# The second head's scores from tokens that are not normed, and block-wise transposes, in a two-block model's expert layer

## The chip, the cores and the metric

The kernel runs on one core of a Trainium2 chip as one launch. The metric is the device time of the run in microseconds (us), the median of several runs. TensorE multiplies matrices and transposes, VectorE (DVE in the profile) and ScalarE (ACT) work on vectors, GpSimd (POOL) issues the gathers of expert rows, and SyncE (SP) issues the loads of weights. All of them run at once and wait for one another through semaphores.

## What is computed

256 tokens of 1024 values pass through two blocks. Both blocks mix the tokens; the second ends with a layer of retrieved experts, and the change touches its beginning. In the reference, cut to what matters:

```
x  = x + gt1 * (concat(mla, mlstm) @ w_out)
h2 = rmsnorm(x, g_norm2) * (1 + sc2) + sh2
x  = x + gt2 * peer(h2, ...)

def peer(h, w_pq, sub_keys, expert_u, expert_v):        # per token
    q = (h @ w_pq).reshape(heads=8, 2, 128)
    s = einsum(q, sub_keys)                              # 2 x 128 scores per head
    sv, si = top_k(s, 16)                                # per half
    best, pos = top_k(sv[0] + sv[1], 16)                 # of 16 x 16 sums
    eidx = (si[0] * 128 + si[1])[pos]                    # 16 experts per head
    g = softmax(best)
    act = gelu(einsum(expert_u[eidx], h))
    return einsum(g * act, expert_v[eidx])
```

So each token has 8 heads with 16 experts each. An expert's row of u and its row of v, 1024 values each, lie side by side in memory.

## The kernel before

**Layout.** `XT` holds the tokens transposed: 8 tiles `k` of 128 features by 256 tokens. For the dot products with gathered rows, tokens must lie on partitions; the kernel calls that form `hn[b]`, one tile of 128 x 1024 for each of the two blocks `b` of 128 tokens. Matrix products at full precision are split in two parts: a weight `w` becomes `wh` (copied by ScalarE, L323) and `wl` (the rest, by VectorE, L268), the tokens become `hh` and `hl`, and `mm3` issues three matmuls for one product. A projection for one head has 2 halves x 8 tiles x 3 = 48 matmuls of 128x256, and its sub-scores are 4 more of 128x128 against the sub-keys (`sk0`, `sk`).

**The first head's way round the norm.** `second` (L1460 to L1516) ends the second block's mixing with `project(1)`, which finishes `XT` two tiles at a time. Behind each it splits these tiles, scaled by the gain only, into `xh` and `xl`. The first head's projection `ua` uses those, so it need not wait for the norm: the scores are linear, so the norm factor `y` of each token is multiplied in afterwards and what the shift adds is computed apart, as a bias. The bias is 16 matmuls of the weights against the shift column (`bp`, fp32) and 2 matmuls against sub-keys (`kp`), before `project(1)` ends. The result goes into a dead part of the constant tile `cst` (`sca0`) by two multiply-adds, which the trace shows as `cst<-s,ny,pc` (L262).

**The expert stage.** `peer` (L1518 to L1790) first finds 8 experts of head 0 in block 0 (`fast`, up to `found`; indices in `eix`), and the gathers begin. Then `normed` writes the normed tokens into a tile `t` that takes one of the 9 buffers `G`, and makes `hh` and `hl` from it; `natural` turns both blocks into `hn` with 32 matmuls against the identity; `scores(1)` follows; `residual` transposes `XT` in 16 transposes into `xn` for the end. `experts` runs 16 rounds (`r`), 16 experts each: round `r` handles head `r % 8` of block `r // 8`. One expert is one indirect DMA of 128 rows of 8 KB (L1685, buffer `G`), a dot product on VectorE (L1689), gelu on ScalarE for four at a time, and, in pieces of 128x512, 2 products of `dg` and `G` on TensorE that accumulate in PSUM. A gather can start when a buffer `G` is free, that is when the products of the expert nine before it are done. `scores(r + 2)` for the next heads is issued in round `r`, the routing of later rounds is handed out between dots (`side`).

**What sets the order.** `at(us)` gives a step a planned time, and a list scheduler orders each engine's instructions by these times and by its own model of when inputs are ready. Weight loads are asked for some time ahead (`wload`, 5 buffers `w`, 3 buffers each for `wh` and `wl`). `tc.issue_after` keeps a step behind another in the order. Each engine and each DMA queue then runs its list strictly in that order.

## Time and profile before

| | |
|---|---|
| median of 3 runs | 1378.23 us (1377.91 to 1381.11) |
| the profiled execution | 1375.42 us |
| its span in the trace | 1373.6 us |
| TensorE busy | 1197.5 us, 87% |
| VectorE busy | 994.4 us, 72% |
| ScalarE busy | 533.6 us, 39% |
| GpSimd busy | 292.5 us, 21% |

The profiled execution is 1.8 us longer than its span and 2.8 us shorter than the median. The shares of busy time are means over stages: in the span's first half TensorE and VectorE alternate, in its second half the DMA engines move the expert rows. The rows below are to be read stage by stage.

### The profile page before, as it was taken

To read this page: it belongs to the slowest core of one execution; us is meant where nothing else is said; L and a number is where in the kernel's file an instruction comes from. 1 tells how busy PE (TensorE), PEld (TensorE's weight loads), DVE (VectorE), ACT (ScalarE), POOL (GpSimd) and SP (SyncE) were. 2 spreads that over 40 slices of the span, in tenths; PEclk is the share of its full clock that TensorE was granted. 3 is DMA by queue.
4 is the path that set the end of the run, shared out by engine and by line. 5 is a ranking of instruction groups with operands and counts; after the bars stand their busy time and mean duration, and the time that the engine had idled before them with its cause. 6 is when DMAs were issued, how large, how long until landed. Compare 5 with 4: busy or idle time off the path is not lost.

```text
span 1373.6 us, 17829 instructions
## 1 busy us (share of the span) xinstructions
PE 1197.5 (87%) x6008; PEld 781.7 (57%) x6008; DVE 994.4 (72%) x2464; ACT 533.6 (39%) x1147; POOL 292.5 (21%) x279
## 2 busy tenths in 40 slices
...
GB/s 333 196 284 270 157 183 173 196 163 260 139 41 100 154 131 77 153 16 36 108 382 381 376 426 428 425 426 361 427 412 426 427 426 418 423 426 404 421 427 275
DMA packets 71483, 387.64 MB, mean 282 GB/s; under 512 B 8417, under 2 KB 9569, under 8 KB 38370
## 3 DMA queue, kind: packets, MB, share of 16 engines
q0 software_dynamic: 36864, 268.45, 46.9%
...
q8 instruction: 48, 0.79, 0.2%
...
HBM read 385.43 MB, written 1.05 MB: 281 GB/s over the span
## 4 chain that ended last, share of the span: by engine, by line
PE 49%; DMA 28%; issue 9%; DVE 8%; POOL 5%; ACT 2%; POOLq 0%; DVEq 0%; SPq 0%; ACTq 0%
DMA G<-uv,eix 23%; PE acc L256 22%; PE acx L256 10%; PE s L256 5%; POOL G L1685 5%; DVE G L1689 3%; PE o L256 2%; DMA wm<-wada 2%; PE c L256 2%; PE c L966 2%; PE t L256 1%; DMA w<-wpq 1%; PE t L259 1%; PE s L412 1%; PE o L645 1%
## 5 line engine op out<-in xcount | busy, mean ns | idle before, releaser
L1689 DVE SCALAR_TENSOR_TENSOR G<-G,hn 128x1024 f32<-128x1024 f32 x256 | 313.4, 1225 | 162.3 <-DMA G<-uv,eix 158.8
L1685 POOL DMA_INDIRECT G<-uv,eix x256 | 284.9, 1113 | 415.6 <-PE o L256 129.5
L323 ACT ACTIVATE wh<-w 128x1024 fp32r<-128x1024 f32 (+2 forms) x140 | 146.4, 1048 | 180.6 <-PE acc L256 111.0
L268 DVE TENSOR_TENSOR wl<-w,wh 128x1024 fp32r<-128x1024 f32 (+2 forms) x140 | 168.8, 1209 | 65.4 <-ACT wh L323 63.8
L256 PE MATMUL t<-G,dg 128*128 128x512 f32 x256 | 149.3, 668 | 62.9 <-ACT dg L1702 62.9
L256 PE MATMUL c<-G,dg 128*128 128x512 f32 x256 | 145.9, 654 | 49.2 <-ACT dg L1702 49.2
L256 PE MATMUL acc<-hh,wh 128*128 128x256 f32 x592 | 173.5, 297 | 6.0 <-ACT hh L468 2.5
L256 PE MATMUL acc<-hh,wl 128*128 128x256 f32 x592 | 173.0, 295 | 2.0 <-DVE wl L268 2.0
L256 PE MATMUL acc<-hl,wh 128*128 128x256 f32 x592 | 164.3, 288 | 1.1 <-DVE hl L268 1.1
L1702 ACT ACTIVATE dg<-cst,w 128x128 f32<-128x128 f32 x256 | 90.1, 395 | 141.7 <-PE acx L256 61.4
L256 PE MATMUL acx<-G,dg 128*128 128x512 f32 x256 | 143.3, 644 | 0.0
L256 PE MATMUL o<-G,dg 128*128 128x512 f32 x256 | 141.1, 635 | 0.0
L1693 ACT ACTIVATE s<-s 128x4 f32<-128x4 f32 (+1 forms) x66 | 13.5, 205 | 306.7 <-DVE G L1689 306.7
L256 PEld LDWEIGHTS t<-G,dg 128*128 128x128 f32 x256 | 50.9, 209 | 142.3 <-ACT dg L1702 87.6
L256 PEld LDWEIGHTS acc<-hh,wh 128*128 128x128 f32 x592 | 115.7, 196 | 14.8 <-issue 4.6
L256 PEld LDWEIGHTS acc<-hh,wl 128*128 128x128 f32 x592 | 115.9, 196 | 8.6 <-issue 4.3
L256 PEld LDWEIGHTS c<-G,dg 128*128 128x128 f32 x256 | 49.5, 206 | 117.0 <-ACT dg L1702 68.5
L262 DVE SCALAR_TENSOR_TENSOR g<-lu,pb,g 128x256 f32<-128x256 f32 x264 | 115.1, 478 | 0.2
L256 PEld LDWEIGHTS acc<-hl,wh 128*128 128x128 f32 x592 | 111.3, 192 | 5.3 <-issue 3.4
L256 PEld LDWEIGHTS acx<-G,dg 128*128 128x128 f32 x256 | 53.5, 209 | 70.7 <-issue 70.7
L256 PEld LDWEIGHTS o<-G,dg 128*128 128x128 f32 x256 | 52.7, 206 | 69.0 <-issue 68.8
L1057 POOL MEMSET lu<- 128x16 f32 x1 | 0.4, 441 | 399.3 <-DVE g L262 399.3
...
## 6 DMA issues: line engine op xcount, KB each, us to landing
w<-w SPq DMA_DIRECT2D x64, 512.0 KB, 4.4
wm<-wada SPq DMA_DIRECT2D x40, 512.0 KB, 4.3
wa<-cw SPq DMA_DIRECT2D x16, 512.0 KB, 5.0
w<-woa SPq DMA_DIRECT2D x16, 512.0 KB, 3.5
w<-wpq SPq DMA_DIRECT2D x14, 512.0 KB, 4.5
w<-w2t SPq DMA_DIRECT2D x12, 512.0 KB, 3.5
w<-wob SPq DMA_DIRECT2D x8, 512.0 KB, 3.5
w<-w2v SPq DMA_DIRECT2D x8, 512.0 KB, 3.8
```

The source lines that it names most:

```text
L256: return pe.matmul(out, lhsT, rhs, start=start, stop=stop)
L259: pe.transpose(out, in_, ident)
L262: return (e or dve).scalar_tensor_tensor(out, a, s, b, op0=op0, op1=op1)
L268: return (e or dve).tensor_tensor(out, a, b, op=op)
L323: act.activation(hi, w, AF.Copy)
L412: pe.matmul(acc[j:j + 32], ones[:, 0:32], sq[:, q] if square else srcs[i + q], start=i + q < 4, stop=i + q >= n - 4, tile_position=(0, j))
L645: pe.matmul(hps[32 * j:32 * j + 32], blk[:, q4 * 4 + j], w[:, j], start=q4 == 0, stop=q4 == 3, tile_position=(0, 32 * j))
L966: pe.matmul(acc[32 * j:32 * j + 32], sc[:, k], w[:, j], start=k == 0, stop=k == 7, tile_position=(0, 32 * j))
L1685: pool.indirect_dma_start(out=G, out_offset=None, in_=A["uv"], in_offset=bass.IndirectOffsetOnAxis(ap=eix[b][:, h, k:k + 1], axis=0))
L1689: dot = dve.scalar_tensor_tensor(G[:, 0:D], G[:, 0:D], 1.0, hn[b], op0=mul, op1=mul, accum_out=s[:, j:j + 1])
L1693: act.activation(s[:, 0:n], s[:, 0:n], AF.Gelu)
L1702: act.activation(dg, ident, AF.Copy, scale=w[:, j:j + 1])
```

## The change

The second head's scores are now computed as the first head's: a bias (16 matmuls against the shift column, 2 against sub-keys; `bias(1, ...)`, with its own load of the two weights, which are loaded once more for the split), a projection of `xh` and `xl` that is placed behind the first head's scores, and two multiply-adds with the norm factor (`rs2`), whose result overwrites the mask part of `cst`. `sk0` holds 4 rows of sub-keys instead of 2. `scores(1)` is gone from `peer`, and `sca` has room for 6 heads.

The first head's two multiply-adds come after all its four sub-score matmuls. The first two splits of the second head's weights stand behind the last split of `XT`.

`normed` returns the normed tokens `t`, with the shift added in place; `halves` makes `hh` and `hl` from them two tiles at a time, behind all of `fast`. `natural(0, tokens)` transposes block 0's tokens directly (8 transposes instead of 16 matmuls), and block 1 is turned by `natural(1)` at round 3 with 16 matmuls. `residual` runs for block 0 at round 2 and for block 1 at round 4, back into the cells of `XT` that it read; `finish` reads them there.

```
@@ -944,3 +944,4 @@
 
-    sca0 = cst[:, CN["cos2"][0]:CN["sin2"][1]].rearrange("p (b q n) -> p b q n", b=2, q=2)
+    sca0 = [cst[:, CN[n][0]:CN[n][0] + 512].rearrange("p (b q n) -> p b q n", b=2, q=2) for n in ("cos2", "cmask")]
+    kb = [None, cst[:, CN["ltri"][0]:CN["utri"][1]].rearrange("p (q n) -> p q n", q=2)]
 
@@ -1460,4 +1461,4 @@
         at(X + 93)
-        sk0 = slot("cw2", 256).rearrange("p (q n) -> p q n", q=2)
-        nc.sync.dma_start(sk0, A["subk"][:, 0:2])
+        sk0 = slot("cw2", 512).rearrange("p (q n) -> p q n", q=4)
+        nc.sync.dma_start(sk0, A["subk"][:, 0:4])
         w0 = [wload(A["wpq"][q], [128, 8, 128], "wm", NWM, b1) for q in range(2)]
@@ -1465,13 +1466,19 @@
         w0l = slot("lu", 2048, F32R).rearrange("p (q k n) -> p q k n", q=2, k=8)
-        bp = psum("s", [128, 2])
-        for q in range(2):
-            for k in range(8):
-                mm(bp[:, q:q + 1], w0[q][:, k], modt[:, 24 + k, 0:1], k == 0, k == 7)
-        b0 = mk(b1, [128, 2], tag="nv4")
-        act.activation(b0, bp, AF.Copy)
-        kp = psum("s", [128, 2, 128])
-        for q in range(2):
-            mm(kp[:, q], b0[:, q:q + 1].broadcast_to([128, 128]), sk0[:, q], True, True)
-        kb = slot("pc", 256).rearrange("p (q n) -> p q n", q=2)
-        act.activation(kb, kp, AF.Copy)
+        kb[0] = slot("pc", 256).rearrange("p (q n) -> p q n", q=2)
+        b0 = mk(b1, [128, 4], tag="nv4")
+
+        def bias(h, w):
+            bp = psum("s", [128, 2])
+            for q in range(2):
+                for k in range(8):
+                    mm(bp[:, q:q + 1], w[q][:, k], modt[:, 24 + k, 0:1], k == 0, k == 7)
+            act.activation(b0[:, 2 * h:2 * h + 2], bp, AF.Copy)
+            kp = psum("s", [128, 2, 128])
+            for q in range(2):
+                i = 2 * h + q
+                mm(kp[:, q], b0[:, i:i + 1].broadcast_to([128, 128]), sk0[:, i], True, True)
+            act.activation(kb[h], kp, AF.Copy)
+
+        bias(0, w0)
+        bias(1, [wload(A["wpq"][2 + q], [128, 8, 128]) for q in range(2)])
         for q in range(2):
@@ -1488,3 +1495,3 @@
                 act.activation(xh[:, k], XT[:, k], AF.Copy, scale=gk)
-                stt(xl[:, k], XT[:, k], gk, xh[:, k].bitcast(F32), mul, sub)
+                last = stt(xl[:, k], XT[:, k], gk, xh[:, k].bitcast(F32), mul, sub)
             at(X + 100 + 2.6 * (n + 1))
@@ -1504,10 +1511,25 @@
                     mm(ua[q], w0h[:, q, k], xl[:, k], False, k == 7)
-        qs = slot("ow", 512).rearrange("p (q t) -> p q t", q=2)
-        for q in range(2):
-            act.activation(qs[:, q], ua[q], AF.Copy)
-        sp = psum("s", [128, 2, 2, 128])
-        for b in range(2):
+
+        def head(h, qs, acc):
+            qs = slot(qs, 512).rearrange("p (q t) -> p q t", q=2)
             for q in range(2):
-                mm(sp[:, b, q], qs[:, q, b * 128:b * 128 + 128], sk0[:, q], True, True)
-            stt(sca0[:, b], sp[:, b], y[:, b:b + 1], kb, mul, add)
+                act.activation(qs[:, q], acc[q], AF.Copy)
+            sp = psum("s", [128, 2, 2, 128])
+            for b in range(2):
+                for q in range(2):
+                    held = mm(sp[:, b, q], qs[:, q, b * 128:b * 128 + 128], sk0[:, 2 * h + q], True, True)
+            return sp, held
+
+        sp, held = head(0, "ow", ua)
+        stt(sca0[0][:, 0], sp[:, 0], y[:, 0:1], kb[0], mul, add)
+        at(X + 116)
+        first_splits.extend([last.ins] * 2)
+        acc = psum("acc", [128, 2, T])
+        for q in range(2):
+            wh, wl = wsplit(A["wpq"][2 + q], [128, 8, 128])
+            with tc.issue_after(held.ins):
+                mm3(acc[:, q], [(wh[:, k], wl[:, k], xh[:, k], xl[:, k]) for k in range(8)])
+        mg["sp"] = head(1, "kv", [acc[:, q] for q in range(2)])[0]
+        at(X + 135)
+        stt(sca0[0][:, 1], sp[:, 1], y[:, 1:2], kb[0], mul, add)
         hh = mk(cp, [128, 8, T], F32R, tag="hh")
@@ -1536,3 +1558,3 @@
         gat = [mk(pp, [128, 8, 16], tag=f"gat{b}") for b in range(2)]
-        sca = mk(pp, [128, 7, 2, 2, 128], tag="sca")
+        sca = mk(pp, [128, 6, 2, 2, 128], tag="sca")
 
@@ -1552,3 +1574,3 @@
                     mm(sp[:, b, q], qs[:, q, b * 128:b * 128 + 128], sk[:, 2 * h + q], True, True)
-            act.activation(sca[:, h - 1], sp, AF.Copy)
+            act.activation(sca[:, h - 2], sp, AF.Copy)
 
@@ -1564,20 +1586,25 @@
                 stt(t[:, k], XT[:, k], mg["pr"][:, k:k + 1], bc, mul, mul)
-                sh = modt[:, 24 + k, 0:1]
-                act.activation(hh[:, k], t[:, k], AF.Identity, bias=sh)
-            for k in range(8):
-                stt(hl[:, k], t[:, k], modt[:, 24 + k, 0:1], hh[:, k].bitcast(F32), add, sub)
+                act.activation(t[:, k], t[:, k], AF.Identity, bias=modt[:, 24 + k, 0:1])
+            return t
 
-        def natural():
+        def halves(t):
+            for k in range(0, 8, 2):
+                act.activation(hh[:, k:k + 2], t[:, k:k + 2], AF.Copy)
+                tt(hl[:, k:k + 2], t[:, k:k + 2], hh[:, k:k + 2].bitcast(F32), sub)
 
-            for b in range(2):
-                for d in range(2):
-                    acc = pst("u", [128, 4, 128])
-                    for k in range(4):
+        def natural(b, t=None):
+
+            bs = slice(b * 128, b * 128 + 128)
+            for d in range(2):
+                acc = pst("u", [128, 4, 128])
+                for k in range(4):
+                    if t is None:
                         for i, x in enumerate((hh, hl)):
-                            last = mm(acc[:, k], x[:, d * 4 + k, b * 128:b * 128 + 128], identr, i == 0, i == 1)
-                    act.activation(hn[b][:, d * 512:d * 512 + 512], acc.rearrange("p a b -> p (a b)"), AF.Copy)
-            return last
+                            mm(acc[:, k], x[:, d * 4 + k, bs], identr, i == 0, i == 1)
+                    else:
+                        tr(acc[:, k], t[:, d * 4 + k, bs], ident)
+                act.activation(hn[b][:, d * 512:d * 512 + 512], acc.rearrange("p a b -> p (a b)"), AF.Copy)
 
         def subscores(h, b, p):
-            return sca0[:, b, p] if h == 0 else sca[:, h - 1, b, p]
+            return sca0[h][:, b, p] if h < 2 else sca[:, h - 2, b, p]
 
@@ -1657,13 +1684,11 @@
 
-        xn = XT.rearrange("p k t -> p (k t)").rearrange("p (b d) -> p b d", b=2)
 
-        def residual(held):
-            xp = [pst("v", [128, 4, 128]) for _ in range(4)]
-            for b in range(2):
-                for k in range(8):
-                    with tc.issue_after(held.ins):
-                        tr(xp[b * 2 + k // 4][:, k % 4], XT[:, k, b * 128:b * 128 + 128], ident)
-            for i in range(4):
-                act.activation(xn[:, i // 2, (i % 2) * 512:(i % 2) * 512 + 512],
-                               xp[i].rearrange("p a b -> p (a b)"), AF.Copy)
+        def residual(b):
+
+            for d in range(2):
+                xp = pst("u", [128, 4, 128])
+                cells = XT[:, 4 * d:4 * d + 4, b * 128:b * 128 + 128]
+                for k in range(4):
+                    tr(xp[:, k], cells[:, k], ident)
+                act.activation(cells, xp, AF.Copy)
 
@@ -1718,4 +1743,6 @@
         with tc.issue_after(found.ins):
-            normed()
-        at(B + 7)
+            tokens = normed()
+            for b in range(2):
+                stt(sca0[1][:, b], mg["sp"][:, b], rs2[:, b:b + 1], kb[1], mul, add)
+        at(B + 3)
         with tc.issue_after(found.ins):
@@ -1723,8 +1750,8 @@
                 placed = ins
-        at(B + 8)
-        held = natural()
-        first_splits.extend([found.ins] * 2)
-        scores(1, B + 9)
-        at(B + 16)
-        residual(held)
+        at(B + 4)
+        natural(0, tokens)
+        at(B + 6)
+        with tc.issue_after(placed.ins):
+            halves(tokens)
+        first_splits.extend([placed.ins] * 2)
 
@@ -1751,3 +1778,4 @@
                 yield 1
-                tt(o, o, xn[:, b, d * 512:d * 512 + 512], add)
+                o4 = o.rearrange("p (k n) -> p k n", k=4)
+                tt(o4, o4, XT[:, 4 * d:4 * d + 4, b * 128:b * 128 + 128], add)
                 nc.sync.dma_start(A["out"][b * 128:b * 128 + 128, d * 512:d * 512 + 512], o)
@@ -1760,2 +1788,8 @@
                 side.append(gate_sums())
+            if r in (2, 4):
+                at(U0 + 16 * PICK * r)
+                residual(r // 2 - 1)
+            if r == 3:
+                at(U0 + 16 * PICK * r)
+                natural(1)
             if r == 10:
@@ -1763,3 +1797,3 @@
             if r < 6:
-                scores(r + 2, U0 + 16 * PICK * r - 12)
+                scores(r + 2, U0 + 16 * PICK * r - (12 if r else -2))
             experts(r % 8, r // 8, U0 + 16 * PICK * r, 4 if r == 0 else 2, (4, 4, 4, 4) if r < 15 else (4, 4, 4, 2, 1, 1))
```

**TensorE, from the end of the mixing to the tokens, before.** `s_7125` are the token sums of the norm, `s_7197` the first head's sub-scores, `t_7250` the spread of the norm factor, and `acc_7317` and `acc_7327` the first of `natural`'s matmuls.

```order
L256 MATMUL s_7125<-cst_62,tmp_7123 128x1 x2
L256 MATMUL s_7197<-cw_1188_6916,ow_7194 128x128 x4
L256 MATMUL t_7250<-dg_7251,cst_62 128x128
L256 MATMUL t_7250<-dg_7254,cst_62 128x128
L256 MATMUL acc_7317<-identr_7213,hh_7204 128x128
L256 MATMUL acc_7327<-identr_7213,hh_7204 128x128
```

**The same place after, its first part.** `s_7151` are the token sums and `s_7223` the first head's sub-scores.

```order
L256 MATMUL o_7171<-g_1202_6979,g_1191_6922 128x256
L256 MATMUL s_7151<-cst_62,tmp_7149 128x1 x2
L256 MATMUL s_7223<-cw_1188_6916,ow_7220 128x128 x4
L256 MATMUL acc_7229<-g_1201_6978,wh_7232 128x256
L256 MATMUL acc_7229<-g_1202_6979,wh_7232 128x256
L256 MATMUL acc_7229<-g_1201_6978,wl_7234 128x256
```

The rows `acc_7229` go on for 48 matmuls, the second head's projection. This is the end of it, and what follows:

```order
L256 MATMUL acc_7229<-g_1202_6979,wh_7262 128x256
L256 MATMUL acc_7229<-g_1201_6978,wl_7264 128x256
L256 MATMUL s_7293<-cw_1188_6916,kv_7290 128x128 x4
L256 MATMUL t_7345<-dg_7346,cst_62 128x128
L256 MATMUL t_7345<-dg_7349,cst_62 128x128
L259 MATMUL acc_7406<-cst_62,G_7352 128x128 x4
L259 MATMUL acc_7412<-cst_62,G_7352 128x128 x3
L256 MATMUL acc_7430<-hh_7299,wh_7433 128x256
```

The spread of the norm factor, `t_7345`, now stands behind 48 matmuls and the second head's sub-scores `s_7293`; `natural`'s matmuls have become 8 transposes, and `acc_7430`, the projection of the third head, follows them.

**TensorE up to the first expert, before.** `acc_7454` is the third head's projection, `acx_7429` are the last of `residual`'s transposes, and `c_7523` is the first expert's first product.

```order
L256 MATMUL acc_7454<-hh_7204,wh_7487 128x256
L256 MATMUL acc_7454<-hl_7205,wh_7487 128x256
L256 MATMUL acc_7454<-hh_7204,wl_7489 128x256
L259 MATMUL acx_7429<-cst_62,XT_61 128x128 x3
L256 MATMUL c_7523<-G_7528,dg_7567 128x512
L256 MATMUL o_7524<-G_7528,dg_7567 128x512
```

**The same place after.** `acc_7717` is the fourth head's projection, `acc_7963` transposes of `residual(0)`, `s_7780` the fourth head's sub-scores, `acc_7969` the fifth head's projection.

```order
L256 MATMUL acc_7717<-hl_7300,wh_7750 128x256
L256 MATMUL acc_7717<-hh_7299,wl_7752 128x256
L259 MATMUL acc_7963<-cst_62,XT_61 128x128 x4
L256 MATMUL s_7780<-sk_7306,qs_7778 128x128 x4
L256 MATMUL acc_7969<-hh_7299,wh_7972 128x256
L256 MATMUL acc_7969<-hl_7300,wh_7972 128x256
L256 MATMUL acc_7969<-hh_7299,wl_7974 128x256
```

19 matmuls of `acc_7969` stand here, and then the first expert, `o_7499`:

```order
L256 MATMUL acc_7969<-hh_7299,wl_7974 128x256
L256 MATMUL acc_7969<-hh_7299,wh_7972 128x256
L256 MATMUL o_7499<-G_7504,dg_7543 128x512
L256 MATMUL t_7500<-G_7504,dg_7543 128x512
L256 MATMUL o_7499<-G_7516,dg_7547 128x512
```

So the list before the first expert holds the third head (48), the fourth (48), 19 of the fifth, and two sets of sub-scores, where it held the second head (48) and the third (48).

**TensorE around the twentieth expert, before.** `c_7523` and `o_7524` are an expert's products, `acc_8473` is the seventh head's projection; the sixth head's last 29 matmuls and the seventh's first 24 stand between the sixteenth expert and the one after it.

```order
L256 MATMUL c_7523<-G_7826,dg_7848 128x512
L256 MATMUL o_7524<-G_7826,dg_7848 128x512
L256 MATMUL c_7523<-G_7831,dg_7852 128x512
L256 MATMUL o_7524<-G_7831,dg_7852 128x512
L256 MATMUL acc_8473<-hh_7204,wh_8506 128x256
L256 MATMUL acc_8473<-hl_7205,wh_8506 128x256
L256 MATMUL acc_8473<-hh_7204,wl_8508 128x256
```

**The same rounds after.** `acc_8493` is the seventh head's projection and `s_8556` its sub-scores; the first `o_7499` here is the seventeenth expert.

```order
L256 MATMUL acc_8493<-hl_7300,wh_8526 128x256
L256 MATMUL acc_8493<-hh_7299,wl_8528 128x256
L256 MATMUL s_8556<-sk_7306,qs_8554 128x128 x4
L256 MATMUL o_7499<-G_7787,dg_7816 128x512
L256 MATMUL t_7500<-G_7787,dg_7816 128x512
L256 MATMUL o_7499<-G_7796,dg_7820 128x512
L256 MATMUL t_7500<-G_7796,dg_7820 128x512
```

From the seventeenth expert on nothing but experts stands in the list for two rounds, where 24 matmuls of `acc_8473` followed the twentieth. The longest block after the first expert is now one of 43 matmuls of the sixth head and 8 of `natural(1)` between the eighth expert and the ninth.

**SyncE's loads around the first gather, before.** `sk` is the table of all sub-keys (1 MB) and `gs` one row; every `w` is half a megabyte of weights.

```order
L314 DMA w_7742<-wpq 128x1024
L1531 DMA sk_7211<-subk 128x2048
L1735 DMA gs_7451<-bgate 1x1024
L314 DMA w_7772<-wpq 128x1024
L314 DMA w_7982<-wpq 128x1024
```

**The same place after.** `w_7230` and `w_7260` are the second head's weights, `w_7970` and `w_8000` the fifth head's.

```order
L314 DMA w_7748<-wpq 128x1024
L314 DMA w_7970<-wpq 128x1024
L1553 DMA sk_7306<-subk 128x2048
L1762 DMA gs_7427<-bgate 1x1024
L314 DMA w_8000<-wpq 128x1024
L314 DMA w_8230<-wpq 128x1024
```

Behind `sk` now stand 7 loads of `wpq` and 8 of `wada`. In the changed kernel the load of `sk` waits until the second head's last matmul (`acc_7229`) has run, since it takes the place of data that this matmul reads.

## Rows read from the trace of the kernel before

**Rows 1.** DMA view, 686.9 to 1373 us: GB/s in 40 slices, queue, issues, us to landing.

```profile
GB/s 373 394 386 377 347 406 426 427 427 427 425 425 427 427 293 427 428 427 395 427 428 426 427 427 427 426 427 409 428 419 427 426 410 398 414 427 428 426 427 136
...
q0 software_dynamic: 36864, 268.45, 94.0%
...
w<-wpq SPq DMA_DIRECT2D x9, 512.0 KB, 7.1
...
w<-wada SPq DMA_DIRECT2D x8, 512.0 KB, 7.7
```

**Rows 2.** Windows: busy us of PE, PEld, DVE, ACT, POOL, PEclk, DMA share, GB/s.

```profile
645.00:676.00 31.00, 31.00 (x244) 28.25 (x244) 20.12 (x46) 15.61 (x28) 0.95 (x1) 1.00 0.27 86
```

**Rows 3.** Timeline of TensorE, first head's bias: start us, us, engine, line, tile.

```profile
643.44 1.84 PE L256 MATMUL s<-modt,wm 128*128 128x1 f32 x16
645.15 0.36 PE L256 MATMUL acc<-g,wh 128*128 128x256 f32 x1
...
647.39 0.61 PE L256 MATMUL s<-cw,nv 128*128 128x128 f32 x4
647.75 0.49 PE L256 MATMUL acc<-g,wh 128*128 128x256 f32 x2
```

**Rows 4.** Timeline of VectorE, from the token sums to the first indices.

```profile
678.00 0.16 DVE L265 TENSOR_SCALAR nv<-s 128x2 f32<-128x2 f32 x1 [3.60 <-PE s L256]
...
680.27 0.48 DVE L262 SCALAR_TENSOR_TENSOR cst<-s,ny,pc 128x256 f32<-128x256 f32 x1
682.07 0.48 DVE L262 SCALAR_TENSOR_TENSOR cst<-s,ny,pc 128x256 f32<-128x256 f32 x1 [1.32 <-PE s L256]
...
685.71 0.17 DVE L262 SCALAR_TENSOR_TENSOR eix<-ij 128x8 uint32<-128x8 f32 x1
```

**Rows 5.** Timeline of GpSimd, gathers 1, 10, 18 and 26 of 256.

```profile
686.95 1.41 POOL L1685 DMA_INDIRECT G<-uv,eix  x1 [35.47 <-PE t L256]
...
718.40 1.86 POOL L1685 DMA_INDIRECT G<-uv,eix  x1 [12.86 <-PE o L256]
...
744.62 0.94 POOL L1685 DMA_INDIRECT G<-uv,eix  x1 [8.70 <-PE o L256]
...
770.43 0.94 POOL L1685 DMA_INDIRECT G<-uv,eix  x1 [7.77 <-DVE G L1689]
```

**Rows 6.** Timeline of SyncE, the load of the sub-key table.

```profile
676.36 0.33 SPq L1531 DMA_DIRECT2D sk<-subk  x1
```

**Rows 7.** Windows as in Rows 2, from the first indices to the thirtieth expert.

```profile
684.00:704.00 20.00, 11.53 (x49) 10.66 (x49) 19.66 (x67) 5.93 (x15) 9.48 (x8) 0.50 0.79 318
704.00:708.00 4.00, 4.00 (x33) 4.00 (x32) 3.19 (x7) 3.41 (x7) 1.18 (x1) 0.92 1.01 428
708.00:792.00 84.00, 84.00 (x422) 57.60 (x421) 64.59 (x178) 35.37 (x66) 30.81 (x27) 1.00 0.96 381
```

**Rows 8.** Windows as in Rows 2, 16 us each, the first experts.

```profile
712.00:728.00 16.00, 16.00 (x83) 10.98 (x82) 14.23 (x52) 7.82 (x15) 5.71 (x5) 1.00 0.94 349
...
744.00:760.00 16.00, 16.00 (x68) 9.76 (x67) 10.49 (x26) 7.01 (x13) 7.15 (x7) 1.00 0.96 368
760.00:776.00 16.00, 16.00 (x88) 11.51 (x87) 12.44 (x37) 4.93 (x12) 5.00 (x5) 1.00 0.86 336
```

**Rows 9.** Timeline of TensorE, transposes, a projection's matmuls, the first two experts, sub-scores.

```profile
701.45 1.07 PE L259 MATMUL c<-cst,XT 128*128 128x128 f32 x4
...
715.68 0.28 PE L256 MATMUL acc<-hl,wh 128*128 128x256 f32 x1
715.80 0.28 PE L256 MATMUL acc<-hh,wl 128*128 128x256 f32 x1
...
716.25 1.02 PE L256 MATMUL c<-G,dg 128*128 128x512 f32 x2
...
719.68 1.05 PE L256 MATMUL s<-sk,qs 128*128 128x128 f32 x8
720.57 1.02 PE L256 MATMUL c<-G,dg 128*128 128x512 f32 x2
```

## The prediction

> **What bounds the kernel now.** I read the DMA view from the first gather on, then the windows ahead of it, then the rows between. From the first gather to the end the DMA engines move 268.45 MB of expert rows and 17 half-megabyte loads (9 of wpq, 8 of wada), mostly at 427 or 428 GB/s [rows 1]. 268.45 MB over 256 gathers is 1.05 MB, at 428 GB/s 2.45 us each; a load of half a megabyte takes 1.22 us. So the second half of the kernel is as long as its bytes, plus the time in which the engines are not full. Such losses stand in five slices at the start and one further on (293) [rows 1]. The first five, each of 17.2 us (686 us over 40), fall short of 428 by 55, 34, 42, 51 and 81 GB/s: 263 / 428 x 17.2 = 10.6 us.
>
> Ahead of the first gather TensorE is the bound: busy 31.00 of 31 us up to 676, at the full clock of 2.4 GHz [rows 2]. VectorE then waits 3.60 us for the token sums and needs 7.7 us more, by way of two multiply-adds, to the first indices [rows 4]; the first gather follows 1.2 us later [rows 5].
>
> Why the early losses: the tenth gather needs a free buffer, so it waits for the first expert's products. It was issued 12.86 us after its queue fell idle, when TensorE had finished what stands ahead of the first expert [rows 5]. From 704 TensorE is busy without a break to 792 [rows 7]: it catches up with experts and the heads' projections, and each long block of projection matmuls holds back buffers. Gather 18 was 8.70 us and gather 26 was 7.77 us late in that way [rows 5], and the windows fall to 349, 368 and 336 GB/s [rows 8]: 16 x (79, 60, 92) / 428 = 3.0, 2.2 and 3.4 us.
>
> **The change part by part.** The sum is made against the profiled execution of 1375.4 us (span 1373.6 and 1.8 outside it); the median of the runs is 2.8 us above it, and I add that at the end.
>
> 1. *The second bias.* 16 matmuls of 128x1 in fp32, which the trace shows as 32 records, and 2 of 128x128. Half of that for the first head went from 643.44 to 645.15, and the two others from 647.39 to 647.75 [rows 3]: 2 x 1.71 + 0.36 = 3.8 us. They stand in the stretch where TensorE has no gap, so nothing hides them: +3.8 us (3.4 if a short gap takes some, 4.6 if a weight comes late once). Their two extra loads and those of the split come while the DMA engines are used to 0.27 [rows 2], and cost nothing there.
>
> 2. *The first head's multiply-adds back to back.* They began at 680.27 and 682.07, the second after a wait of 1.32 for TensorE [rows 4]. All four sub-score matmuls are now done during the norm, so the second starts 0.48 after the first: -1.3 us (0 if the matmuls come late, -1.4 at most). The first gather moves by 3.8 - 1.3 = +2.5 us, to 689.5.
>
> 3. *Bytes behind the first gather.* 15 loads are left where 17 were: -2.4 us. But the sub-key table, as large as two loads, was issued at 676.36, long ahead [rows 6]; now it waits for the second head's 48 matmuls. With 0.12 us for each [rows 9] they end about 682 + 5.8 = 688, so 1 us of it passes before the first gather and 1.4 us after. Net -1.0 us (0 if all of it falls behind, -2.4 if none).
>
> 4. *What TensorE does before the first expert.* It now holds the third head (48), the fourth (48), 19 of the fifth, 8 transposes and two sets of sub-scores. 115 x 0.12 = 13.8; 4 transposes took 0.87 at half clock [rows 9, 7], 8 at full clock then 0.9; a set of sub-scores 0.89 [rows 9]: together 16.5 us. They start when VectorE has made the first low halves. The spread of the norm factor is issued behind the second head's block and sub-scores, at about 690; 8 multiply-adds of 0.48 each, as long as those of 128x256 in [rows 4], the copies of two tiles, their low halves and one weight's split of some 3 us in all follow one another. That puts the start at about 698. At full clock the first expert would then start at 714.5. But the granted clock was 0.50 from 684 to 704, with TensorE busy in 11.53 of 20 us, and rose only in 704 to 708 [rows 7]. The start of the new list is as broken, so I take the same again: half speed to about 708, 5 us lost, and the start at 719.5, where it was 716.25 [rows 9]. The tenth gather moves by +3.3 us to 721.7. The first batch on the DMA engines (9 gathers, 3 loads and the rest of the table, where it was 9 and 5) ends 1 us later than now, so 2.3 us more are idle (0 to 3.5).
>
> 5. *After the first expert.* An expert takes (719.68 - 716.25) / 2 = 1.72 us of TensorE [rows 9]. Up to the seventeenth expert the list now has 125 projection matmuls, 16 for block 1's tokens, 8 transposes, 3 sets of sub-scores: 15.0 + 1.8 + 0.9 + 2.7 = 20.4 us besides the experts. It had 168 matmuls and 5 sets, 20.2 + 4.5 = 24.7 us, and 24 matmuls more behind the twentieth. The block of 53 matmuls (29 and 24) between the sixteenth and seventeenth experts becomes 22, and the 24 vanish: the loss of 3.4 us in 760 to 776 goes. The one of 744 to 760 stays: 43 matmuls and 8 of block 1's tokens stand together between the eighth and ninth experts, 6 us and more. So -3.4 us (0 if the late start moves the loss, -5.6 if both go).
>
> 6. *The rest.* A multiply-add pair for the second head and transposes in another place run under transfers. The last slices hold what they held; the late loss (293) comes from the last head's weights, whose order is unchanged. 0.
>
> *A rule on the clock.* The rows show transposes at half clock before 704 and none alone at full clock [rows 9, 7]. The Trainium skill, in TensorE: Matmul & The Clock Gate, Part 4: PE-mode transpose, says that transposes don't count as busy for the clock as matmuls do; since 8 transposes replace 16 matmuls of block 0's tokens, the clock would rise later still, and the sum by it is the slow rival's. The trace agrees so far only that the clock stayed low with mixed work; it shows no stretch of transposes alone.
>
> Sum: 2.5 - 1.0 + 2.3 - 3.4 = +0.4 us. The rows behind term 5 are the least sure; half of the second loss going too (1.1) would be as near to them as none, so I take -0.7: 1374.7 for a profiled run, 1377.5 by the median.
>
> **The rivals.** *Faster.* The second head's block keeps TensorE busy to 688, some 6 us longer than now, so the clock may not fall before the third head begins; then the first expert starts when its weights are ready (four dots, gelu), about 717, term 4 is zero, and both losses behind it go: 2.5 - 1.0 + 0 - 5.6 = -4.1, and up to -6 with less lost in 712 to 728; between them 1373.5. For it: the stretch in which TensorE is now half idle [rows 7] begins later. Against: VectorE still sets when the low halves come, and TensorE is idle for it.
>
> *Slower.* The mechanism is the first expert's start. TensorE is cold until 710 and the start comes at 721 or later; the tenth gather waits 1.5 us longer than I took, and since TensorE has no slack until the projections are done, the block between the eighth and ninth experts stalls the buffers as much as the two blocks did: term 5 is zero. 2.5 - 1.0 + 3.5 = +5.0: 1383.2. It decides from a first expert later than about 721. For it: 16.5 us of work stand where 96 matmuls and 16 transposes stood, 13.3 by the same rows, and VectorE says when they start. Against: 48 matmuls fewer in all.
>
> *It does nothing to what counts.* The second head is not needed before the seventeenth expert, so having it early buys no gather; what is gained is only TensorE's time later. That is my forecast's case: front and gain cancel.
>
> **How the numbers follow.** A difference of 0.3%, 4.1 us, is about what a measurement of this kernel can tell from none. No change within that: 0.46, at 1377.5. Faster: 0.30, at 1373.5 or below. Slower: 0.24, at 1383 or above. The range runs from 1371.5 (the fast rival's -6 and half of the 1.4 us that term 3 leaves open) to 1383.5 (the slow rival); beyond either end I leave 1 in 10.
>
> **What would show it.** Right: first gather at 689 to 690; matmuls of the second head at 682 to 688 and the sub-key load at 688; first expert at 718 to 721; no window below 380 GB/s in 760 to 780; TensorE's break without gaps ended some 8 us sooner than 792. Wrong: a gap of TensorE ahead of the token sums (a late weight), a first expert before 717 or after 722, a new late gather between the eighth and ninth experts of more than 10 us, or a change at the far end, in the last 20 us.

## The result and the profile after

The changed kernel takes 1383.97 us, the median of 14 runs (1378.36 to 1391.00), against 1376.44 for the kernel before in the same comparison (14 runs, 1371.64 to 1381.11). The ratio is 1.0053, with a 95% interval of 1.0035 to 1.0072: slower by 7.3 us, where 0.3% or 4.1 us can be told from nothing. The forecast was 1377.5 with a range of 1371.5 to 1383.5. The median lies just beyond its slow end, and the sign is the one that the forecast thought least likely.

The profiled execution of the changed kernel took 1380.3 us (span 1378.2), 3.7 us less than the median of its runs. Up to the load of the first head's weights, which SyncE issued at 632.17 us before and at 632.73 after, the changed kernel differs only by its two loads for the second bias (575.17) and by two loads of another weight (`wo`) that it puts off to 653.23. So 0.56 us of every difference below stood there already.

**The second bias.** The timeline of TensorE shows its records in four pieces, and the two matmuls against the sub-keys:

```profile
648.47 0.95 PE L256 MATMUL s<-modt,w 128*128 128x1 f32 x8
654.12 0.28 PE L256 MATMUL s<-modt,w 128*128 128x1 f32 x2
654.59 1.17 PE L256 MATMUL s<-modt,w 128*128 128x1 f32 x10
656.90 1.40 PE L256 MATMUL s<-modt,w 128*128 128x1 f32 x12
661.49 0.60 PE L256 MATMUL s<-cw,nv 128*128 128x128 f32 x4
```

They are the 32 records that the forecast counted, in a stretch without a gap, as [rows 2, 3] had it; a window over the same times as [rows 2] (busy us of PE, PEld, DVE, ACT, POOL, granted clock, DMA share, GB/s):

```profile
645.00:676.00 31.00, 31.00 (x249) 28.82 (x249) 19.70 (x48) 14.12 (x27) 0.00 (x0) 1.00 0.34 120
```

**From the token sums to the first gather.** Timelines of VectorE, SyncE and GpSimd; the gathers are numbers 1, 10 and 26 and answer to [rows 5]:

```profile
683.36 0.16 DVE L265 TENSOR_SCALAR nv<-s 128x2 f32<-128x2 f32 x1 [1.94 <-PE s L256]
685.64 0.88 DVE L262 SCALAR_TENSOR_TENSOR cst<-s,ny,pc 128x256 f32<-128x256 f32 x2
689.68 0.17 DVE L262 SCALAR_TENSOR_TENSOR eix<-ij 128x8 uint32<-128x8 f32 x1
```

```profile
690.06 0.33 SPq L1553 DMA_DIRECT2D sk<-subk  x1
```

```profile
690.92 1.08 POOL L1710 DMA_INDIRECT G<-uv,eix  x1 [141.73 <-DMA gs<-bgate]
...
724.14 0.94 POOL L1710 DMA_INDIRECT G<-uv,eix  x1 [11.75 <-PE t L256]
...
776.67 1.71 POOL L1710 DMA_INDIRECT G<-uv,eix  x1 [8.19 <-DVE tmp L1647]
```

The two multiply-adds now run back to back (0.88 us for both, where [rows 4] has a wait of 1.32 between them): from the token sums' factor to the first indices it is 6.32 us, where it was 7.71. The factor itself comes 5.36 us later, and the first gather 3.97. From there on the lag grows to 5.7 us at the tenth gather and 6.2 at the twenty-sixth; the last one was issued at 1350.59 before and 1356.61 after, 6.0 us later. Of these 6.0 us, 4.0 are there before the first gather.

**The first expert and the windows behind it.** Timeline of TensorE, then windows as in [rows 8]:

```profile
721.98 1.02 PE L256 MATMUL o<-G,dg 128*128 128x512 f32 x2
```

```profile
712.00:728.00 16.00, 15.75 (x103) 12.64 (x102) 16.00 (x48) 9.17 (x19) 2.91 (x4) 1.00 0.85 337
...
760.00:776.00 16.00, 14.34 (x52) 8.32 (x53) 12.58 (x37) 3.94 (x10) 4.11 (x4) 0.90 0.92 375
776.00:792.00 16.00, 12.64 (x30) 5.36 (x29) 9.71 (x26) 3.10 (x10) 9.87 (x8) 0.99 0.81 323
```

The loss that [rows 8] shows at 760 to 776 (336 GB/s) did not go. It moved one window on: 323 GB/s at 776 to 792, where the kernel before had 420, is 16 x 105 / 428 = 3.9 us, and 760 to 776 still loses 16 x 53 / 428 = 2.0. TensorE has gaps there now (12.64 of 16 us), as forecast, but no gather came of them.

So the profile says that most of the loss arises ahead of the first gather, where the only new work is the second bias. Its 3.4 us of issue don't make 7.3, though, and this execution was 3.7 us faster than the median. What the other executions had is for the experiments to say.

### The profile page after: what moved, and what is told of

It reads as the page before. It is cut to its first block, busy times and chain, and to the rows that moved or that the text cites. A ratio compares the mean times of both kernels' runs of the same rounds, so it can differ in the third digit from the quotient of the medians.

```text
span 1378.2 us, 17893 instructions
## 1 busy us (share of the span) xinstructions
PE 1189.8 (86%) x6036; PEld 778.4 (56%) x6036; DVE 994.4 (72%) x2462; ACT 535.3 (39%) x1153; POOL 291.3 (21%) x279
## 4 chain that ended last, share of the span: by engine, by line
PE 50%; DMA 25%; issue 9%; DVE 8%; POOL 5%; ACT 2%; POOLq 0%; DVEq 0%; SPq 0%; ACTq 0%
DMA G<-uv,eix 22%; PE acc L256 22%; PE acx L256 11%; PE s L256 6%; POOL G L1710 5%; DVE G L1714 4%; PE o L256 2%; PE t L256 2%; DMA wm<-wada 2%; PE c L967 2%; PE c L256 1%; PE s L412 1%; PE t L259 1%; PE o L645 1%; PE o L811 1%
## 5 line engine op out<-in xcount | busy, mean ns | idle before, releaser
L256 PE MATMUL acc<-hh,wh 128*128 128x256 f32 x576 | 169.4, 297 | 7.1 <-ACT hh L468 2.5
L256 PE MATMUL acc<-hh,wl 128*128 128x256 f32 x576 | 169.6, 297 | 2.3 <-DVE wl L268 2.3
L256 PE MATMUL acc<-hl,wh 128*128 128x256 f32 x576 | 160.3, 289 | 2.5 <-DVE hl L268 2.5
L256 PE MATMUL c<-G,dg 128*128 128x512 f32 x256 | 140.5, 632 | 0.0
L256 PE MATMUL t<-G,dg 128*128 128x512 f32 x256 | 138.2, 623 | 0.0
L256 PEld LDWEIGHTS acx<-G,dg 128*128 128x128 f32 x256 | 50.0, 205 | 146.1 <-ACT dg L1727 94.1
L256 PEld LDWEIGHTS o<-G,dg 128*128 128x128 f32 x256 | 48.8, 202 | 128.9 <-ACT dg L1727 80.4
L256 PEld LDWEIGHTS c<-G,dg 128*128 128x128 f32 x256 | 52.3, 204 | 68.2 <-issue 68.2
```

What stands on the lines that cost most here:

```text
L256: return pe.matmul(out, lhsT, rhs, start=start, stop=stop)
```

## The experiments

Each kernel ran 6 to 14 times beside the kernel before; ratios are against that. The kernel before had a median of 1376.44 us beside the changed kernel, 1376.39 beside e1 to e4, 1375.33 beside e5 to e8, 1376.92 beside e9 to e12 and 1377.01 beside e13 to e15. Prices in us below are ratios times that, unless a profile is named; the difference of the medians can be another (e13: 24.1 us by its ratio, 21.8 by the medians). Each kernel was profiled once.

| kernel | sets of one-column bias matmuls | median us | ratio, 95% interval |
|---|---|---|---|
| after | 2 | 1383.97 | 1.0053 (1.0035 to 1.0072) |
| e1 second head early, blocks as before | 2 | 1385.36 | 1.0066 (1.0041 to 1.0091) |
| e2 block by block, second head as before | 1 | 1378.66 | 1.0023 (1.0001 to 1.0044) |
| e3 before, adds together | 1 | 1379.01 | 1.0025 (1.0005 to 1.0046) |
| e4 after, second bias left out | 1 | 1374.89 | 0.9993 (0.9974 to 1.0013) |
| e5 before, first bias twice | 2 | 1384.97 | 1.0068 (1.0043 to 1.0092) |
| e6 after, token halves first | 2 | 1384.17 | 1.0053 (1.0033 to 1.0073) |
| e7 after, second bias behind the first head's scores | 2 | 1384.39 | 1.0055 (1.0033 to 1.0077) |
| e8 e6 and e7 together | 2 | 1382.50 | 1.0056 (1.0036 to 1.0076) |
| e9 after, both biases 128 columns wide | 0 (2 wide) | 1382.48 | 1.0035 (1.0013 to 1.0057) |
| e10 before, bias twice, 128 wide | 0 (2 wide) | 1381.95 | 1.0032 (1.0013 to 1.0052) |
| e11 before, bias 128 wide | 0 (1 wide) | 1377.28 | 0.9997 (0.9978 to 1.0015) |
| e12 before, first bias left out | 0 | 1377.60 | 0.9990 (0.9970 to 1.0010) |
| e13 before, bias four times | 4 | 1398.86 | 1.0175 (1.0146 to 1.0205) |
| e14 before, bias four times, 128 wide | 0 (4 wide) | 1385.35 | 1.0070 (1.0044 to 1.0095) |
| e15 after, both biases early in the mixture | 2, elsewhere | 1388.14 | 1.0090 (1.0058 to 1.0121) |

### Which part carries the loss: e1, e2, e3, e4

e1 is the changed kernel with `normed`, `natural`, `residual`, `finish` and their calls as in the kernel before. e2 is the reverse, the kernel before with those parts from the change. e3 takes one line of the kernel before out of its loop:

```
         for b in range(2):
             for q in range(2):
                 mm(sp[:, b, q], qs[:, q, b * 128:b * 128 + 128], sk0[:, q], True, True)
+        for b in range(2):
             stt(sca0[:, b], sp[:, b], y[:, b:b + 1], kb, mul, add)
```

e4 is the changed kernel with 14 of the second head's 16 bias matmuls left out:

```
-                for k in range(8):
-                    mm(bp[:, q:q + 1], w[q][:, k], modt[:, 24 + k, 0:1], k == 0, k == 7)
+                for k in range(8 if h == 0 else 1):
+                    mm(bp[:, q:q + 1], w[q][:, k], modt[:, 24 + k, 0:1], k == 0, k == 7 or h == 1)
```

> The second head early as in the changed kernel (bias, projection behind the first head, adds), but tokens, halves, natural and residual as in the kernel before. Theory H (what is paid is the work put ahead of the first gather: second bias 3.6 us, 48 matmuls ahead of the norm factor's spread): first gather 690 to 691, tenth gather about 722, time 4 to 7 us above before. Theory B (what is paid is the block-wise part, whose halves come behind the whole first routing): tenth gather at 718 to 720 although the first gather is late, time within 3 us of before.

> Tokens and residual block by block as in the changed kernel, second head in the expert stage as before (one bias). Theory H: first gather at 687, first expert no later than 717, time 0 to 4 us below before, since 16 matmuls and 16 transposes leave the list ahead of the first expert. Theory B: first low halves at 698 or later, first expert 719 or later, time 3 to 7 us above before.

> The kernel before with one edit: the first head's two multiply-adds stand behind all four sub-score matmuls. Both theories: indices and first gather 1.3 us earlier (685.6). If what moves the first gather moves the end, 1.3 us less in time (0.1%); if the tenth gather decides, which waits for TensorE's list and not for the first gather, no change in time.

> The changed kernel with 2 of the 16 bias matmuls of the second head instead of 16 (the other 14 are left out; everything else stands). Theory H: first and tenth gather 3.2 us earlier than in the changed kernel, time 3 us below it. Theory B: the first gather is 3.2 us earlier, the tenth by 0 to 1, since VectorE's list of halves and splits sets it; time within 1.5 us of the changed kernel.

Measured: e1 1.0066, e2 1.0023, e3 1.0025, e4 0.9993. The early second head alone costs all of the loss; without 14 matmuls, the whole change is at the time of the kernel before. That is 8.3 us below the changed kernel, where the two theories had 3 us and under 1.5: the set costs more than its 3.4 us of issue. The two parts that were to help don't help by themselves, and e2 has the early first expert of its theory H (714.14 us) but not its time. e3 has its lead in the profile (6.32 us from the token sums' factor to the indices, as in the changed kernel) and not in its time. Twelve runs each leave e2 and e3 between 0 and 0.46% slower, so a small loss can't be excluded; a gain can.

e2 shows where a gain goes. Timeline of GpSimd, gathers 1, 10 and 26:

```profile
686.87 1.08 POOL L1688 DMA_INDIRECT G<-uv,eix  x1 [35.14 <-PE t L256]
...
711.05 0.96 POOL L1688 DMA_INDIRECT G<-uv,eix  x1 [7.32 <-PE o L256]
...
770.98 0.94 POOL L1688 DMA_INDIRECT G<-uv,eix  x1 [9.46 <-PE o L256]
```

Its tenth gather is 24.18 us behind the first, where [rows 5] has 31.45: 7.3 us won. Its twenty-sixth is 84.11 us behind, where [rows 5] has 83.48. All of it is given back within 16 gathers: TensorE still owes the same projections, and from 760 to 776 e2 moves 277 GB/s, where [rows 8] has 336, with TensorE busy in 15.75 of 16 us.

e4 also judges the slow rival, whose mark was a first expert later than 721. Gathers 1 and 10 of e4 and its first expert:

```profile
694.30 1.08 POOL L1710 DMA_INDIRECT G<-uv,eix  x1 [138.21 <-DMA gs<-bgate]
...
727.47 0.94 POOL L1710 DMA_INDIRECT G<-uv,eix  x1 [15.15 <-DVE wl L268]
```

```profile
725.32 1.02 PE L256 MATMUL o<-G,dg 128*128 128x512 f32 x2
```

The first expert comes 31.0 us behind the first gather, as in the changed kernel (721.98 - 690.92 = 31.1), and the tenth gather 33.2 us behind it in both. So e4 has the late first expert in full, and its runs are not slow. (The profiled execution, 1380.55 us, is the slowest of e4's twelve. It reached the load of the first head's weights, which all kernels share, at 639.86, 7.7 us later than the one of the kernel before, so only distances within it are compared.)

### Whether the order around it matters: e6, e7, e8

e6 makes the halves of the tokens as soon as the first experts are found, ahead of block 0's transposes (`issue_after(found.ins)` in place of `placed.ins`). e7 moves one line of the changed kernel, the second bias, behind the first head's sub-scores; e8 does both:

```
-        bias(1, [wload(A["wpq"][2 + q], [128, 8, 128]) for q in range(2)])
...
+        at(X + 115)
+        with tc.issue_after(held.ins):
+            bias(1, [wload(A["wpq"][2 + q], [128, 8, 128]) for q in range(2)])
         at(X + 116)
```

> The changed kernel, but the low halves may come as soon as the first indices are found, as in the kernel before, and not behind the whole first routing. If the late halves (first at 701.6) hold back the third head's projection and with it all that TensorE has to catch up: first halves near 697, first expert 2 to 4 us earlier, gather 34 as much earlier, time 2 to 4 us below the changed kernel. If only the front counts: within 1.5 us of it.

> The changed kernel, but the second bias stands behind the first head's scores, where TensorE had idle time, and no longer ahead of the token sums. If the work ahead of the first gather is what is paid: first gather 3.5 us earlier than in the changed kernel, the spread of the norm factor where it was, time 2 to 4 us below the changed kernel. If it only moves within the same stretch of TensorE (the spread waits for it): tenth gather as in the changed kernel and no change in time.

> Both edits, halves first and the second bias behind the first head's scores. If both holds are real and add up: 5 to 8 us below the changed kernel, so at the time of before or up to 2 us below it.

Measured: 1.0053, 1.0055 and 1.0056, the changed kernel's own ratio each time; none of the gains came. e7 was built so that the matmuls no longer stand ahead of the token sums, from which the first gather follows. They don't: its first gather came 53.28 us behind the shared load, before 54.78. But its tenth came 38.55 us behind the first, where [rows 5] has 31.45, and the loss is the same. Its timeline of TensorE shows the first sight of the cause; the start, the busy time and the count of records stand in each row:

```profile
687.51 3.85 PE L256 MATMUL s<-modt,w 128*128 128x1 f32 x32
...
691.58 0.63 PE L256 MATMUL acc<-g,wh 128*128 128x256 f32 x2
692.01 0.41 PE L256 MATMUL acc<-g,wl 128*128 128x256 f32 x1
```

```profile
691.32:695.32 4.00, 4.00 (x25) 4.00 (x24) 0.57 (x4) 1.23 (x2) 2.11 (x3) 0.64 0.81 235
```

Right behind the 32 one-column records the projection's matmuls take 0.21 us from start to start (691.58 to 692.01 for two), where they take 0.12 at full clock [rows 9]. The window has the granted clock at 0.64, with TensorE busy in 4.00 of 4.00 us.

### The set by itself, one column or 128: e5, e10, e9, e11, e12

e5 is the kernel before with the first bias issued twice, and nothing else. e10 is the same in another form: the shift's column is read 128 times as the moving operand, so the matmuls are 128 columns wide, and one column of the result is kept.

```
-        for q in range(2):
+        for q in (0, 0, 1, 1):
             for k in range(8):
-                mm(bp[:, q:q + 1], w0[q][:, k], modt[:, 24 + k, 0:1], k == 0, k == 7)
+                mm(bp[:, q], w0[q][:, k], modt[:, 24 + k, 0:1].broadcast_to([128, 128]), k == 0, k == 7)
```

e9 gives both biases of the changed kernel that form, e11 the one of the kernel before. e12 leaves out 14 of the 16 matmuls of the kernel before (`range(1)` in place of `range(8)`).

> The kernel before with the 16 bias matmuls of the first head issued twice (the second time over the first result), so 3.4 us more of TensorE in the stretch without gaps ahead of the first gather, and the rest of the order almost unchanged. If a delay of the first gather is paid whole: first and tenth gather 3.4 us later, time 3 to 4 us above before. If the expert stage makes it up: under 1.5 us.

> The kernel before, with the first head's 16 bias matmuls issued twice, each 128 columns wide. With one column this cost 0.68%. Theory of the clock: 3.5 us of issue at most, less what the first set's own falls of the clock cost before, so a ratio of 1.000 to 1.003, and no window between the modulation's last matmuls and the first gather in which TensorE is busy throughout at a clock of 0.50. Rival (the price is in the matmuls): 1.0068 again.

> The kernel after, with both heads' bias matmuls made 128 columns wide instead of one: the moving operand is the shift's column read 128 times, and one column of the result is kept. The count of matmuls, their weights and their place are unchanged. Theory (one-column matmuls let TensorE's granted clock fall, as in the profile of the first bias issued twice, where it was 0.50 for 8 us with TensorE busy 4.00 of 4 us): the second bias costs its issue time of 3.5 us alone, so 1374.9 + 3.5, about 1378.4 us, ratio 1.002. Rival (the price is in the 16 more matmuls, their weight loads and what their order moves, not in the clock): as the kernel after, 1384 us, ratio 1.0053. If the wide form were dearer to issue, slower still.

> The kernel before, with its one set of bias matmuls made 128 columns wide. Theory of the clock: the same or up to 2 us faster, since one set of 16 seldom lets the clock fall there (1.00 throughout in the profile of before), ratio 0.998 to 1.000. Rival (wide matmuls cost more, the clock nothing): 1.000 to 1.002.

> The kernel before with 14 of the first head's 16 bias matmuls left out, so its first head's scores lack most of their bias. It prices the first set as the run without the second bias priced the second. If every set costs what the second does (issue and a fall of the clock in some executions): 7 to 9 us faster, ratio 0.994. If only a second set is dear, since two sets stand within 10 us of one another: 3 us faster, 0.998.

Measured: e5 1.0068, as dear as the whole change, where its expectation had 4 us at most. Windows of e5, four microseconds each, over the bias:

```profile
643.89:647.89 4.00, 4.00 (x31) 3.79 (x29) 3.62 (x11) 3.18 (x10) 0.00 (x0) 1.00 0.02 4
647.89:651.89 4.00, 4.00 (x31) 4.00 (x31) 2.71 (x14) 0.30 (x3) 0.00 (x0) 0.81 0.00 0
651.89:655.89 4.00, 4.00 (x20) 4.00 (x20) 2.64 (x8) 0.00 (x0) 0.95 (x1) 0.50 0.00 0
655.89:659.89 4.00, 4.00 (x20) 4.00 (x20) 0.12 (x1) 0.00 (x0) 0.00 (x1) 0.50 0.00 0
```

TensorE is busy throughout, and its clock falls to 0.50, the lower of its two levels (1.2 GHz), for 8 us and more: 20 records a window where there were 31 and more. e10's windows at the same times, where the same weights meet 128 columns:

```profile
647.90:651.90 4.00, 4.00 (x37) 4.00 (x37) 2.97 (x15) 0.32 (x3) 0.00 (x0) 1.00 0.00 0
651.90:655.90 4.00, 4.00 (x36) 4.00 (x35) 2.43 (x8) 0.00 (x0) 0.95 (x1) 1.00 0.00 0
```

The timelines of TensorE show that the wide form is not dearer to issue. The first 24 records of e5, then those of e10, with the record that follows each:

```profile
647.59 2.73 PE L256 MATMUL s<-modt,wm 128*128 128x1 f32 x24
650.18 0.40 PE L256 MATMUL acc<-g,wh 128*128 128x256 f32 x1
```

```profile
647.62 2.84 PE L256 MATMUL s<-modt,wm 128*128 128x128 f32 x24
650.22 0.37 PE L256 MATMUL acc<-g,wh 128*128 128x256 f32 x1
```

In the runs the wide form costs 1.0032 (e10) and 1.0035 (e9), against 1.0053 to 1.0068 for six kernels with two one-column sets. The intervals of any single pair overlap, so this was still to be settled; for the changed kernel itself (1.0035 to 1.0072, and e9 1.0013 to 1.0057) it stays so. Both fit a set's issue time of 3.4 us or 0.25%. e11 and e12, at 0.9997 and 0.9990, came out as the kernel before: the first set, alone, has no price that these runs resolve. For e12 the case in which every set costs what the second does (0.994) is excluded; its other case, 3 us faster (0.998), is not.

### Four sets: e13, e14

The kernel before with the bias issued four times, in the one-column and in the wide form; the diffs are those of e5 and e10 with `(0, 0, 0, 0, 1, 1, 1, 1)`.

> The kernel before, with the first head's 16 bias matmuls (one column wide) issued four times. Theory (each one-column set costs 3.4 us of issue and lets TensorE's granted clock fall in part of the executions): at least three times what the second set cost, 20 to 25 us, ratio 1.015 to 1.018, and a stretch at a clock of 0.50 with TensorE busy throughout in the profile. Rival (a set costs its issue alone, the rest of the second set's price was chance): 3 x 3.4, about 10 us, ratio 1.0075, the same as the wide form.

> The kernel before, with the first head's 16 bias matmuls issued four times, each 128 columns wide. Theory: issue alone, 3 x 3.4, about 10 us, ratio 1.0075, at a clock of 1.00 from the first of them to the last residual matmul. Rival (the price is per matmul, whatever its width): as the one-column form, whatever that is.

Measured: 1.0175 and 1.0070, and the intervals are far apart. The same weights, the same count and the same place cost 24.1 us in one form and 9.6 us in the other, 8.0 and 3.2 us for each further set. The windows of e13, then of e14, over the first part of the sets:

```profile
648.00:652.00 4.00, 4.00 (x21) 4.00 (x21) 1.81 (x10) 0.00 (x0) 0.00 (x0) 0.51 0.00 0
652.00:656.00 4.00, 4.00 (x21) 4.00 (x21) 1.83 (x6) 0.00 (x0) 0.95 (x1) 0.50 0.00 0
656.00:660.00 4.00, 4.00 (x20) 4.00 (x21) 0.87 (x2) 1.06 (x1) 0.00 (x0) 0.50 0.00 0
```

```profile
648.00:652.00 4.00, 4.00 (x36) 4.00 (x35) 1.73 (x4) 1.30 (x2) 0.95 (x1) 1.00 0.00 0
652.00:656.00 4.00, 4.00 (x37) 4.00 (x36) 4.00 (x7) 2.43 (x4) 0.00 (x0) 1.00 0.52 164
```

A profile gives the price without the spread of the runs, from the load that all kernels share (SyncE) to the first gather (GpSimd). In turn before, e13 and e14:

```profile
632.17 1.26 SPq L314 DMA_DIRECT2D wm<-wpq  x2
```

```profile
634.21 1.26 SPq L314 DMA_DIRECT2D wm<-wpq  x2
...
707.39 1.40 POOL L1685 DMA_INDIRECT G<-uv,eix  x1 [52.97 <-PE t L256]
```

```profile
630.41 1.26 SPq L314 DMA_DIRECT2D wm<-wpq  x2
...
695.70 1.41 POOL L1685 DMA_INDIRECT G<-uv,eix  x1 [45.96 <-PE t L256]
```

With the first gather of [rows 5] at 686.95, that is 54.78 us before, 73.18 in e13 and 65.29 in e14. Three further sets cost 10.5 us at full clock, 3.5 each, and 18.4 us with the clock falling, 6.1 each. The 3.5 us are the forecast's term 1; the rest is the clock.

The executions that were not profiled say the same. Each run lists its mean granted clock: 0.936 over the six runs of e13, 0.945 over the ten of e14 and 0.945 over the sixteen of the kernel before. As the lower level is half of the upper, 2 x (1 - clock) x span is the time at the lower one, by the runs' own numbers 178.8 us in e13 and 151.5 before (estimates; the spread of the runs leaves some 5 us either way on the difference). The 27.3 us more cost about half of that where TensorE is the bound, 13.6 us; with 10.5 us of issue that makes the 24.1 of the runs. The profiled execution of e13 has the highest clock of its six (0.941), so its 18.4 us are at the low end.

### Where TensorE seemed to have time: e15

The changed kernel with both biases moved ahead into the mixture (`at(X + 60)`), with loads of their own. The place was chosen as one where TensorE was busy in 10.1 of 16 us in the profile of before, at 608 to 624. That was misread: 10.11 is the column of its weight loads (PEld), and its matmuls fill 15.32 of 16 us, so there was no gap to use.

```profile
608.00:624.00 16.00, 15.32 (x72) 10.11 (x71) 10.16 (x39) 10.45 (x32) 0.00 (x0) 0.89 0.01 2
```

```
+        at(X + 60)
+        for h in range(2):
+            bias(h, [wload(A["wpq"][2 * h + q], [128, 8, 128]) for q in range(2)])
...
-        bias(0, w0)
-        bias(1, [wload(A["wpq"][2 + q], [128, 8, 128]) for q in range(2)])
+        spread_bias(0)
+        spread_bias(1)
```

> The kernel after, with both heads' bias matmuls (one column wide) moved ahead, into the mixture stage, where TensorE was busy 10.1 of 16 us at 608 to 624 us in the profile of before; the weights for them are loaded there once more. Nothing else is changed. Theory (the second bias is dear because it stands where TensorE has no idle time): as the kernel after without the second bias, 1375 us, ratio 0.999, and up to 3 us below that for the first set. Rival (the time goes elsewhere in the change): as the kernel after, 1384 us, 1.0053.

Measured: 1.0090, slower than the change itself, which neither theory had: the price is in the set, as the first said, but the place was no gap, and the matmuls did not even land there. The scheduler put the matmuls not at 608 to 624 but at 586, ahead of work that the next steps wait for. Timeline of TensorE in e15, then the row at which the kernel before began that same work:

```profile
586.32 9.18 PE L256 MATMUL s<-modt,w 128*128 128x1 f32 x52 [1.29 <-DVE g L268]
595.36 2.06 PE L256 MATMUL s<-g,wa 128*128 128x512 f32 x2
```

```profile
586.93 1.13 PE L256 MATMUL s<-g,wa 128*128 128x512 f32 x2 [1.49 <-DVE g L268]
```

52 records in a row took 9.18 us, 0.18 each where 0.11 is full speed (2.73 us for 24 in e5), and the next matmuls took 2.06 us instead of 1.13. The windows of e15 show the clock fall while nothing but one-column matmuls ran:

```profile
588.00:592.00 4.00, 4.00 (x24) 4.00 (x23) 0.82 (x1) 0.00 (x0) 0.00 (x0) 0.58 0.51 144
592.00:596.00 4.00, 4.00 (x18) 3.83 (x18) 1.22 (x1) 1.11 (x2) 0.00 (x0) 0.50 0.72 258
```

The shared load that stands at 630 to 641 us in the other profiles came at 645.57. Against the pause ahead of 586.32 as the cause speaks the kernel before, where a pause of 1.49 us stands there too and the clock stayed at 1.00 from 584 to 612. From the shared load to the end e15 takes 740.4 us (1386.0 - 645.57), the kernel before 741.4 (1373.6 - 632.17): with the sets gone from there, nothing of the loss is left behind that load, as far as one profile of each can tell. It is the clearest sight of the fall in these traces. Whether the change would be free with the bias in a real gap was not tried.

## Why the prediction was wrong, step by step

**Term 1, the second bias: mis-sized, and the larger part of the error.** The count, the place and the issue time were right: the 16 matmuls took 3.4 us in the profile and 3.5 a set in e14, as forecast (2 x 1.71; 3.8 with the two against the sub-keys). The upper bound of 4.6 was wrong. The step that failed is the sentence that took the duration of [rows 3] as the price, with a late weight as the only way to pay more. Those rows ran at a granted clock of 1.00. The matmuls that follow are the same at either level but take 0.12 or 0.21 us, and a one-column set can change the level. Priced by the runs, the set costs 8.0 us (e13, a third of 24.1) or 8.3 (1.0053 against e4's 0.9993, of 1376). That the part beyond the issue time is the clock's is shown in the kernel before, by e13 against e14. For the changed kernel it is carried over from there: its own profile has no fall, and e9 does not settle it.

Why the profile of the changed kernel shows the clock at 1.00 there is known only in part. In the one profile of each kernel, the fall stands at the second set in e1, e5, e7 and e8, and not in the changed kernel and e6. Yet e1, e6 and the changed kernel issue that set in the same four pieces at the same distances, so the program's order alone does not decide it. The changed kernel's profiled execution lies 3.7 us below its median, at a mean granted clock of 0.951 where its 14 runs have 0.946, as one without the fall should. In the four profiles with wide sets and in e12 the clock is 1.00 from the shared load to the last matmul of `project(1)`. The Trainium skill, in TensorE: Matmul & The Clock Gate, under What's actually happening, says that the gate goes by how busy the array has recently been. The trace agrees only if busy means something other than the profile's busy time: in e13 that is 12.00 of 12 us at a clock of 0.51 and 0.50.

**Term 2, the multiply-adds: right.** 1.39 us less from the factor to the indices, forecast 1.3. In the runs of e3 it can't be seen: a lead of 1.4 us is below what they tell.

**Term 3, bytes behind the first gather: wrong, small.** The forecast had 1 us of the sub-key load's 2.4 pass ahead of the first gather. It was issued at 690.06, 0.86 us ahead of the gather, so nearly all of it passes behind: 0, not -1.0, the end of the term's own range.

**Term 4, the first expert: its place nearly right, in part by luck.** The list was to start at about 698 and to lose 5 us at half speed up to about 708. The granted clock was 0.50 in the last window before the list ran through:

```profile
696.73:700.73 4.00, 2.28 (x6) 1.01 (x6) 3.86 (x20) 4.00 (x10) 3.07 (x4) 0.62 1.00 420
700.73:704.73 4.00, 2.64 (x9) 2.05 (x10) 4.00 (x11) 0.21 (x3) 0.00 (x0) 0.50 1.01 426
```

But the third head's matmuls waited for VectorE's low halves, and ran without a break only from 703.47:

```profile
702.42 0.80 PE L256 MATMUL acc<-hl,wh 128*128 128x256 f32 x2 [1.05 <-DVE hl L268]
```

That is 12.6 us behind the first gather, where 8.5 were forecast. Full pace came at 707.9, so some 20 matmuls went at 0.21 us instead of 0.12: by estimate 2 us lost, not 5. The two errors cancel but for 1 us. The first expert came 31.1 us behind the first gather (forecast 30.0, before 29.3), and the tenth gather 33.2 (forecast 32.2, before 31.5). What the lag costs is not settled. In the changed kernel's profile 2.0 us of it are still there at the last gather (665.69 us behind the first, before 663.64). But e4, with the same lag, is as fast as before: its thirty-fourth gather comes 99.28 us behind its first, in the kernel before 101.25. In e4 and e2, late and early at the tenth, the gathers are level with the kernel before at the twenty-sixth (83.28 and 84.11 against 83.48).

**Term 5, the loss after the first expert: wrong.** It moved from 760 to 776 into 776 to 792 and kept its size (3.4 and 3.9 us, with 2.0 left behind). The forecast read gather 26 of [rows 5] as held by projection matmuls, but its row names VectorE's dot product (L1689), and in the changed kernel VectorE's search (L1647, 8.19 us). What a gather needs by the program is its buffer, here the products of the seventeenth expert, which ended at 776.40, as that search did (776.43). A row of ScalarE, and a window as in [rows 2]:

```profile
769.94 0.60 ACT L1570 ACTIVATE qs<-acc 128x512 f32<-128x512 f32 x1 [7.55 <-PE acc L256]
```

```profile
772.00:776.00 4.00, 3.28 (x4) 1.49 (x5) 3.93 (x12) 1.25 (x4) 0.00 (x0) 0.60 0.85 354
```

ScalarE's gelu for that expert (770.43) stood in its list behind the copy of a head's queries, which waited 7.55 us for the projection. And behind the gaps that TensorE now had its clock fell (0.60 in that window), so that expert's first product took 2.06 us (772.72), where [rows 9] has 1.02. So fewer projection matmuls between two experts did not by themselves release a gather.

**Together.** Terms 2 to 5 were to give -3.4 us, or -4.5 as taken. Without the second bias they give 0.9993, that is -1.0 us, with an interval of -3.6 to +1.8: the sum as worked lies just inside, the one taken outside. So of the 8.0 us between the forecast difference (-0.7) and the measured one (+7.3), 4.5 are term 1 (8.3 for 3.8) and 3.5 the gains that did not come, term 5 above all. The forecast also stood on 1378.23 us for the kernel before, which measured 1376.44 beside the changed kernel; in plain times its error looks 1.8 us smaller than it is.

**The rivals.** The slow one named the time to within a microsecond (1383.2), its mark came true (721.98, later than 721) and its term 5 was zero. It is still not what happened: e4 keeps its mechanism and is not slow, e5 has none of it and is as slow as the change. A rival can be right in its number and wrong in its cause, and only a run that keeps the mechanism without the rest shows it. The fast rival's price, a clock that stays up, did not occur at the third head (0.62 and 0.50 above). The third case, that an early second head buys no gather, is borne out by e4, which has that head early and is at the time of before.

**What stays open.** Why the first set has no price that the runs resolve: e12 at 0.9990 (0.9970 to 1.0010) against a second set's 8 us. Its issue alone (0.998) lies within that interval; its profile reached the first gather 2.3 us sooner than before, of 3.4 that the set takes. Nor does the first set always leave the clock alone: in the profiles of e1, e2, e3 and e8 it fell behind the first half of that set (0.79 and 0.79 in the two windows of e2 from 634.80 to 642.80), in those of before, after, e4, e6 and e7 it did not. In the runs that were not profiled, the clock is known only as a mean over the span, so where it fell in them is not shown. For the changed kernel the means don't settle it either: 0.946, and 0.947 in e4, where single runs lie between 0.939 and 0.958.
